# Modulation products of a two-block network: 19 longer runs on TensorE in place of 25, used ahead of their loads' place

## The chip, the cores and the metric

The kernel runs on one core of one Trainium2 chip. The metric is the time of one execution on the device, in microseconds; the figure for the kernel before is the median of three runs.

## The reference, cut to what matters

Two blocks follow each other, each of two layers, on 256 tokens of width 1024. The first is a hybrid of three attentions; the second a hybrid of a convolution, a gated linear attention and a softmax attention, over the 256 tokens and 256 context tokens. Only the second block has a modulation:

```python
def hybrid_layer_2(xs, cs, c, c_ctx, norm_g, w_mod, b_mod, ...):
    shift_x, scale_x, gate_x = jnp.split(jax.nn.silu(c) @ w_mod + b_mod, 3, axis=-1)
    shift_c, scale_c, gate_c = jnp.split(jax.nn.silu(c_ctx) @ w_mod + b_mod, 3, axis=-1)
    hx = rms_norm(xs, norm_g) * (1 + scale_x[:, None]) + shift_x[:, None]
    hc = rms_norm(cs, norm_g) * (1 + scale_c) + shift_c
...
    xs = xs + gate_x[:, None] * merge(px, ya_x, yb_x, yc_x)
```

`w_mod` is 1024 by 3072 in float32 for each of the two layers, 25 MB together, and it meets only two vectors (`c` and `c_ctx`). The vectors are inputs, so these products depend on nothing else in the network and can be made at any time before their results are needed: layer 0's shift and scale before the second block's first normalisation, its gate at that layer's end, layer 1's three later still.

## The kernel before, in words

All other weights come through a stream (`WStream`): a table lists the units, 512 KB each as a rule, in the order of use. A unit is loaded by SyncE's DMA queue into one of four raw buffers (`_dma`, tag `wraw`, line 130), then split by ScalarE (a cast, line 154, giving `wh`) and VectorE (a subtraction, line 155, giving `wl`) into two float32r parts in one of five pairs of buffers (`_split`). Each product of the layers is three matmuls, `mm3` (lines 184 to 186): high by high, high by low, low by high. `get(key)` hands out a split unit and first calls `ahead`, which writes loads for `ad` and splits for `asp` entries of the table ahead of the current one (3 and 2 at first, 6 and 3 from unit 0O00 on).

A unit's name has the layer and the step: in the first block A to I are the input projections and O the output, in the second block AKV, AQ and BQ (attention), Va and Vb (convolution values), GK, GQ, GV, ag, gg, m1 to m3 (gates) and oa, og, oc, o (outputs). 1A2 is the third unit of layer 1's step A.

The modulation weights are 48 more units of that table, in float32 and without a split: layer l, third s (0 shift, 1 scale, 2 gate), k of eight 128-row blocks, 128 by 1024 each, 512 KB. `mod_stream` (line 762) is a generator that makes one unit's products per step. In a unit, four matmuls (line 770) share the moving weights' four quarters of 256 columns among four column groups of the array: the stationary operand is 32 columns wide (128*32 in the trace), and quarter q goes to partitions 32q to 32q+31 of one PSUM accumulator, which is held over the eight units of a third (tag `gm`, five banks for all products of that kind). After the eighth unit ScalarE copies the accumulator out (line 775), two small matmuls against a selection matrix transpose it (line 778, `modt`), and VectorE adds the bias (line 782), and for the scale multiplies with the norm's gain. In the trace each of these float32 matmuls has two records.

`FILL` says where: before unit 1B2 two steps, before 1E2 three, and so on, 25 runs of one to five units, in the order layer 0 scale, shift, gate, then layer 1. In the table the modulation units of a run stand directly ahead of the unit whose `get` makes them.

The order of instructions on an engine is the framework's: it takes ready instructions by the order in which the program wrote them, by a model of their times, so work written later can be placed inside a run and a run inside other work. A manual dependency (`g.wait`) makes an instruction wait for another; `g.after` only fixes an order. A buffer is given to its next owner when all users of the last one are done, and SyncE's queue issues its loads strictly in order.

Of the kernel before, what the change touches and what calls it, by code (L numbers as in the profile page):

```python
# [3 lines left out]

# [6 lines left out]
F32 = mybir.dt.float32  # L11
# [4 lines left out]
OP = mybir.AluOpType  # L16
# [13 lines left out]
TG = 2  # L30
# [8 lines left out]

MORDER = (1, 0, 2)  # L40

FILL = '1B2 2 1E2 3 1D2 3 1F0 2 1G0 2 1H2 1 0Va0 2 0Va1 2 0Va2 2 0GV0 1 0ag0 2 0ag2 2 1GV0 3 1ag0 2 1ag2 2 1A0 1 0BQ2 2 1F2 2 1GK0 1 1B0 1 1A3 5 1C2 1 0ag1 1 1H0 1 0GK0 2'

# [9 lines left out]
def units1():  # L55
    c = lambda *ns: [SPL1[n] for n in ns]
    u = {}
    for key, cols in (('A', c(*_A)), ('B', c('idx_q')), ('C', c('diff_q')), ('D', c('diff_k')), ('E', c('diff_v')),
                      ('H', [(3276, 512)]), ('I', [(3788, 512)])):
        u[key] = [(f'{key}{j}', 2 * j, 2, cols) for j in range(4)]  # L60
    u['A'] = [(f'A{j}', KA[j], KA[j + 1] - KA[j], c(*_A)) for j in range(len(KA) - 1)]
    u['F'] = [(f'F{2 * i + m}', 0, 8, [(SPL1[n][0] + 128 * m, 128)])
              for i, n in enumerate(('fox_q', 'fox_k')) for m in range(2)]
    u['G'] = [(f'G{j}', 4 * j, 4, c('fox_v')) for j in range(2)]
    return [e for st in STEPS[0].split() if st in u for e in u[st]]


def units1o():
    return [(f'O{c}{j}', 2 * j, 2, [(512 * c, 512)]) for c in range(2) for j in range(4)]


def ncols(cols):
    return sum(n for _, n in cols)
# [20 lines left out]
def unit_table(prefix, units, base):  # L94
    t = []
    for key, _, kk, cols in units:
        n = ncols(cols)
        t.append((prefix + key, base, kk, n))
        base += 128 * kk * n
    return t, base  # L100
# [10 lines left out]
class WStream:  # L111
# [46 lines left out]
    def whole(self, key):  # L158

        i = self.idx[key]  # L160
        self.ahead(i)
        key, src, off, kk, n = self.table[i]
        return self.raw.pop(i).rearrange("p (k n) -> p k n", k=kk)

    def ahead(self, i):
        while self.nd < min(len(self.table), i + self.ad + 1):
            self._dma()
        while self.ns < min(len(self.table), i + self.asp + 1):
            if self.table[self.ns][0] in self.f32:
                self.ns += 1  # L170
            else:
                self._split()

    def get(self, key):
        self.ad, self.asp = self.looks.pop(key, (self.ad, self.asp))
        for _ in range(self.fills.pop(key, 0)):
            next(self.stream)
        i = self.idx[key]
        self.ahead(i)
        return self.spl[i]  # L180

# [551 lines left out]
def units_mod():  # L733
    return [(f'mod{s}{k}', k, 1, [(D * s, D)]) for s in MORDER for k in range(8)]
# [24 lines left out]
TAPG = ((0, 0, 6, 4), (3, 3, 14, 10))  # L759


def mod_stream(g, l, W):

    nc, sp, pp = g.nc, g.sp, g.pp
    for s in MORDER:
        ps = pp.tile([128, 256], F32, name=f'mod{l}{s}', tag='gm', bufs=g.GM)
        for k in range(8):
            w = W.whole(f'{l}mod{s}{k}')
            for q in range(4):
                nc.tensor.matmul(ps[32 * q:32 * q + 32], g.cz[:, k // 2, 2 * (k % 2):2 * (k % 2) + 32],  # L770
                                 w[:, 0, 256 * q:256 * q + 256], start=k == 0, stop=k == 7)
            if k < 7:
                yield
        r = sp.tile([128, 256], F32, name=f'modr{l}{s}', tag='tg', bufs=TG)
        nc.scalar.copy(r, ps)
        pt = pp.tile([128, 2, 4, 2], F32, name=f'modt{l}{s}', tag='at', bufs=g.AT)
        for i in range(2):
            nc.tensor.matmul(pt[:, i].rearrange("p q w -> p (q w)"), r[:, 128 * i:128 * i + 128], g.sel8,
                             start=True, stop=True)
        ks = slice(8 * s, 8 * s + 8)  # L780
        v = lambda t: t.rearrange("p (q i) w -> p q i w", q=4)
        nc.vector.tensor_add(v(g.mod[l][:, ks, :]), pt.rearrange("p i q w -> p q i w"),
                             v(g.bmod[l][:, ks, None].to_broadcast([128, 8, 2])))
        if s == 1:

            nc.vector.scalar_tensor_tensor(g.modA[l], g.mod[l][:, ks, :], 1.0,
                                           g.ng[l][:, :, None].to_broadcast([128, 8, 2]), op0=OP.add, op1=OP.mult)
        yield


# [42 lines left out]
def new_hT(g, l):  # L833
    return [[g.k8([128, 4, 512], f'hT{s}{i}_{l}', F32R) for i in range(2)] for s in 'hl']
# [874 lines left out]
def table(src, prefix, units):  # L1709
    t, _ = unit_table(prefix, units, 0)  # L1710
    return [(k, src, o, kk, n) for k, o, kk, n in t]
# [12 lines left out]
def program(ctx, tc, ins, out, parts=(1, 2)):  # L1724
    g = setup(ctx, tc, ins)
    nc = g.nc
    mods = sum((table(ins[f'wm_{l}'], f'{l}', units_mod()) for l in range(2)), [])
    f32 = {e[0] for e in mods}
    fs = FILL.split()
    fills = {k: int(n) for k, n in zip(fs[::2], fs[1::2])}  # L1730
    seq = []
    if 1 in parts:
        for l in range(2):
            us = units1()
            if l == 0:
                seq += [(f'0{k}', None, 0, kk, ncols(c)) for k, _, kk, c in us[:len(KA) - 1]]
                us = us[len(KA) - 1:]
            seq += table(ins[f'w1_{l}'], f'{l}', us) + table(ins[f'w1o_{l}'], f'{l}', units1o())
    for l in range(2):
        t2 = tables2(ins, l)  # L1740
        o = [t2[f'{l}{k}'] for k in order2(l)]
        if l == 0:

            o = o[:7] + [(f'0BQ{i}', *e[1:]) for i, e in enumerate(o[3:7])] + o[7:]
            o += [(f'0p{i}', *e[1:]) for i, e in enumerate(o[-8:])]
        seq += o
    tab, m = [], 0
    for e in seq:
        n = fills.get(e[0], 0)
        tab += mods[m:m + n] + [e]  # L1750
        m += n
    assert m == len(mods)
    ls = LOOK.split()
    looks = {k: (int(a), int(b)) for k, a, b in zip(ls[::3], ls[1::3], ls[2::3])}
    W = WStream(g, tab, looks, f32, fills)
    W.stream = itertools.chain(mod_stream(g, 0, W), mod_stream(g, 1, W))

    xsp = g.dram.tile([128, 2048], F32, name='xsp')

    def loaded(src, nm, key=None):  # L1760

        t = g.k8([128, 8, 256], nm)
        d = nc.sync.dma_start(t, src.rearrange("p (k t) -> p k t", k=8))
        if key is not None:
            g.after(d, W.loads.get(key, W.last))
        return t

    def spill(t):
        nc.sync.dma_start(xsp.rearrange("p (k t) -> p k t", k=8), t)

    def load_res():
        return loaded(xsp, 'xT', '0o1'), loaded(ins['ctxt'], 'ctxT', '0o1')
    hT0 = []

    def ctx_prep():
        hT0.extend(new_hT(g, 0))
        norm_prep(g, 0, [(loaded(ins['ctxt'], 'ctx0', HOOK[2] if 1 in parts else None), 0)], hT0, 0, 256)

    def x_prep(tb, c, pt):

        x = g.t2([128, 4, 128], f'npx{tb}{c}')
        for i in range(4):
            k = 4 * c + i
            if i in NPA:
                nc.scalar.activation(x[:, i], pt[:, i], AF.Identity, scale=g.modA[0][:, k, 1:2], bias=g.mod[0][:, k, 1:2])
            else:
                nc.vector.tensor_scalar(x[:, i], pt[:, i], g.modA[0][:, k, 1:2], g.mod[0][:, k, 1:2],
                                        op0=OP.mult, op1=OP.add)
        hh, hl = (t[c][:, :, 256 + 128 * tb:384 + 128 * tb] for t in hT0)
        nc.scalar.copy(hh, x)  # L1790
        nc.vector.tensor_sub(hl, x, hh.bitcast(F32))
    if 1 in parts:
        xTh, xTl = load_x(g, ins, W)
        setup1(g, ins, W)
        W.hooks[HOOK[3]] = lambda: setup_mod(g, ins, W)
        st = block1(g, 0, xTh, xTl, lambda: load_xtok(g, ins, W), W, False)
        block1(g, 1, *st, W, True, ctx_prep, spill, x_prep)
    setup2(g, ins)
    rope2_tables(g, 0)
    hT1 = []  # L1800

    def then(xT):
        hT1.extend(new_hT(g, 1))
        norm_prep(g, 1, [(xT, 1)], hT1, 0, 256)
    xT, cT = block2(g, 0, hT0, load_res, W, then=then)
    rope2_tables(g, 1)
    norm_prep(g, 1, [(cT, 0)], hT1, 0, 256)
    block2(g, 1, hT1, lambda: (xT, None), W, out=out)
# [22 lines left out]
```

## Time and profile before

| | |
|---|---|
| median of three runs | 1191.99 us (1191.82 to 1192.95) |
| the profiled execution | 1192.62 us |
| its span | 1190.8 us |
| TensorE busy | 1168.5 us, 98% |
| VectorE, ScalarE busy | 921.1 us, 569.5 us |
| DMA | 171.33 MB, 144 GB/s on average |

Busy time of TensorE is the union of modelled intervals: a matmul's row begins at its issue and ends when its result is written, so rows overlap and the cost of an instruction is read from the distance between starts. PE is TensorE's matmuls, PEld its weight loads, DVE VectorE, ACT ScalarE, SP SyncE.

### The profile page before, as it was taken

What the parts mean: (1) busy time and instruction counts of PE and PEld (TensorE: products, weight loads), DVE (VectorE), ACT (ScalarE), POOL (GpSimd) and SP (SyncE); (2) the same over time, 40 slices, a digit from 0 to 9 for tenths busy, and PEclk for the clock granted to TensorE, in tenths of its full rate; (3) what the DMA queues carried; (4) which work ended last, traced back from release to release, by engine and by line L of the source; (5) the groups of instructions that cost most, each with busy time, mean ns of one, the idle gap of its engine ahead of it and who ended that gap; (6) DMA issues with size and microseconds to landing.
All of it is one profiled execution on the core that took longest, in us unless ns stands there. A gap on an engine that the chain in (4) does not pass through costs nothing.

```text
span 1190.8 us, 20632 instructions
## 1 busy us (share of the span) xinstructions
PE 1168.5 (98%) x8024; PEld 975.7 (82%) x8024; DVE 921.1 (77%) x2051; ACT 569.5 (48%) x1024; POOL 11.2 (1%) x42
## 2 busy tenths in 40 slices
PE   8999999999999999999999999999999999999998
PEld 6788777677887777767887888888999778999998
DVE  6996766967799859989545986755799897896984
ACT  5556634456555433247444422433455534855552
POOL 0000000000000000000000000000000000000000
PEclk9999999999999999999999999999999999999999
DMA  7634566465555642024221232325545333554552
GB/s 263 224 125 127 186 207 225 155 229 195 177 194 181 230 137 89 19 73 145 68 84 59 89 100 78 106 89 177 178 142 186 96 107 123 179 162 127 174 176 72
DMA packets 47538, 171.33 MB, mean 144 GB/s; under 512 B 5260, under 2 KB 5900, under 8 KB 46672
## 3 DMA queue, kind: packets, MB, share of 16 engines
q1 hardware_dynamic: 47440, 170.01, 43.7%
q8 instruction: 63, 1.03, 0.3%
q14 instruction: 35, 0.29, 0.1%
HBM read 167.89 MB, written 2.10 MB: 143 GB/s over the span
## 4 chain that ended last, share of the span: by engine, by line
PE 76%; DVE 11%; DMA 6%; ACT 5%; issue 2%; SPq 0%; ACTq 0%; DVEq 0%
PE f0m L186 3%; PE f0m L185 3%; PE f0m L184 3%; PE f1m L186 2%; PE f1m L184 2%; PE f1m L185 2%; PE po L185 1%; PE po L186 1%; PE po L184 1%; PE mod L770 1%; PE go L186 1%; PE go L185 1%; PE go L184 1%; PE yog L186 1%; PE yoc L186 1%
## 5 line engine op out<-in xcount | busy, mean ns | idle before, releaser
L1012 DVE SCALAR_TENSOR_TENSOR ucv<-up,par,ucv 128x512 f32<-128x512 f32 (+1 forms) x240 | 147.3, 614 | 2.8
L184 PE MATMUL f0m<-hTh,wh_0m 128*128 128x512 f32 x192 | 75.1, 391 | 0.0
L185 PE MATMUL f0m<-hTl,wh_0m 128*128 128x512 f32 x192 | 75.1, 391 | 0.0
L186 PE MATMUL f0m<-hTh,wl_0m 128*128 128x512 f32 x192 | 74.8, 390 | 0.0
L184 PE MATMUL f1m<-hTh,wh_1m 128*128 128x256 f32 x192 | 54.9, 286 | 0.1
L186 PE MATMUL f1m<-hTh,wl_1m 128*128 128x256 f32 x192 | 54.8, 286 | 0.0
L185 PE MATMUL f1m<-hTl,wh_1m 128*128 128x256 f32 x192 | 54.5, 284 | 0.0
L154 ACT CAST wh_0m<-wr_0m 128x1024 fp32r<-128x1024 f32 x24 | 25.1, 1047 | 55.9 <-PE f0m L185 14.5
L155 DVE TENSOR_TENSOR wl_0m<-wr_0m,wh_0m 128x1024 fp32r<-128x1024 f32 x24 | 29.3, 1222 | 18.2 <-ACT wh_0m L154 18.1
L184 PEld LDWEIGHTS f0m<-hTh,wh_0m 128*128 128x128 f32 x192 | 36.1, 188 | 7.4
L185 PEld LDWEIGHTS f0m<-hTl,wh_0m 128*128 128x128 f32 x192 | 36.1, 188 | 7.3
L186 PEld LDWEIGHTS f0m<-hTh,wl_0m 128*128 128x128 f32 x192 | 36.1, 188 | 7.3
L184 PEld LDWEIGHTS f1m<-hTh,wh_1m 128*128 128x128 f32 x192 | 36.8, 191 | 0.5 <-ACT wh_1m L154 0.3
L186 PEld LDWEIGHTS f1m<-hTh,wl_1m 128*128 128x128 f32 x192 | 36.7, 191 | 0.2 <-DVE wl_1m L155 0.2
L185 PEld LDWEIGHTS f1m<-hTl,wh_1m 128*128 128x128 f32 x192 | 36.8, 191 | 0.1
L154 ACT CAST wh_1m<-wr_1m 128x1024 fp32r<-128x1024 f32 x24 | 24.9, 1049 | 24.4 <-PE f1m L185 7.6
L155 DVE TENSOR_TENSOR wl_1m<-wr_1m,wh_1m 128x1024 fp32r<-128x1024 f32 x24 | 29.3, 1221 | 8.6 <-ACT wh_1m L154 8.4
L155 DVE TENSOR_TENSOR wl_0o<-wr_0o,wh_0o 128x1024 fp32r<-128x1024 f32 x8 | 9.8, 1224 | 13.2 <-ACT wh_0o L154 13.2
L1413 DVE SCALAR_TENSOR_TENSOR xT<-po,mod,xT 128x256 f32<-128x256 f32 x16 | 7.7, 483 | 14.3 <-PE po L186 14.3
L185 PE MATMUL po<-mgl,wh_0o 128*128 128x256 f32 x64 | 18.2, 285 | 0.0
L186 PE MATMUL pp<-mgh,wl_0p 128*128 128x256 f32 x64 | 18.2, 284 | 0.0
L185 PE MATMUL pp<-mgl,wh_0p 128*128 128x256 f32 x64 | 18.2, 284 | 0.0
(1857 smaller groups left out, 3960.6 us busy)
## 6 DMA issues: line engine op xcount, KB each, us to landing
wr_0mod<-in_wm_dram SPq DMA_DIRECT2D x24, 512.0 KB, 4.5
wr_1mod<-in_wm_dram SPq DMA_DIRECT2D x24, 512.0 KB, 3.7
wr_0m<-in_w_dram SPq DMA_DIRECT2D x24, 512.0 KB, 3.5
wr_1m<-in_w_dram SPq DMA_DIRECT2D x24, 512.0 KB, 3.5
wr_0O<-in_w1o_dram SPq DMA_DIRECT2D x8, 512.0 KB, 3.6
wr_1O<-in_w1o_dram SPq DMA_DIRECT2D x8, 512.0 KB, 3.6
wr_0o<-in_wo_dram SPq DMA_DIRECT2D x8, 512.0 KB, 3.6
wr_0p<-in_wo_dram SPq DMA_DIRECT2D x8, 512.0 KB, 3.7
```

Source lines behind the costliest of these rows:

```text
L154: g.nc.scalar.copy(wh, r)
L155: g.nc.vector.tensor_sub(wl, r, wh.bitcast(F32))
L184: nc.tensor.matmul(out, lh, rh, start=start, stop=False)
L185: nc.tensor.matmul(out, lh, rl, start=False, stop=False)
L186: nc.tensor.matmul(out, ll, rh, start=False, stop=stop)
L770: nc.tensor.matmul(ps[32 * q:32 * q + 32], g.cz[:, k // 2, 2 * (k % 2):2 * (k % 2) + 32], w[:, 0, 256 * q:256 * q + 256], start=k == 0, st ...
L1012: yield nc.vector.scalar_tensor_tensor(o, src, dw[:, i, j:j + 1], o, op0=OP.mult, op1=OP.add)
L1413: nc.vector.scalar_tensor_tensor(r[:, f, :], ps[:, :256], g.mod[l][:, 16 + f, w:w + 1], r[:, f, :], op0=OP.mult, op1=OP.add)
```

## The change

The 48 units are taken in 24 pairs, the two of a pair being the same k of two thirds (`MODS`: scale and shift of layer 0; gate of layer 0 and scale of layer 1; shift and gate of layer 1). A pair's eight matmuls fill the two halves of one accumulator of 512 columns, so there are three accumulators, copies and groups of transposes (eight records, four matmuls) in place of six. The list of runs has 19 entries, 14 of one pair and 5 of two. In the table a run's loads now stand one or two units behind the unit whose `get` makes the products. `get` issues the loads up to the run's last one and hands that load to the generator, and the first matmul of the run waits for it. `ahead` counts only units that are split, so modulation units no longer use up the look-ahead, and `whole` no longer calls it.

```diff
-FILL = '1B2 2 1E2 3 1D2 3 1F0 2 1G0 2 1H2 1 0Va0 2 0Va1 2 0Va2 2 0GV0 1 0ag0 2 0ag2 2 1GV0 3 1ag0 2 1ag2 2 1A0 1 0BQ2 2 1F2 2 1GK0 1 1B0 1 1A3 5 1C2 1 0ag1 1 1H0 1 0GK0 2'
+FILL = (('1A2', 1, 1), ('1B1', 1, 1), ('1E0', 1, 1), ('1E3', 1, 1), ('1C2', 1, 1), ('1D2', 1, 1), ('1F1', 1, 1), ('1H0', 1, 1), ('0BQ3', 1, 2), ('0Va2', 1, 2), ('0Va3', 1, 1), ('0GK0', 1, 1), ('0GQ1', 2, 2), ('0GV2', 2, 2), ('0ag1', 2, 2), ('0ag3', 1, 1), ('0m3_3', 1, 1), ('0m3_6', 1, 1), ('0gg1', 1, 1))
+MODS = (((0, 1), (0, 0)), ((0, 2), (1, 1)), ((1, 0), (1, 2)))
...
     def whole(self, key):
 
         i = self.idx[key]
-        self.ahead(i)
+        while self.nd <= i:
+            self._dma()
...
+    def behind(self, i, n):
+
+        while n and i < len(self.table) - 1:
+            i += 1
+            n -= self.table[i][0] not in self.f32
+        return i
+
     def ahead(self, i):
-        while self.nd < min(len(self.table), i + self.ad + 1):
+        while self.nd < min(len(self.table), self.behind(i, self.ad) + 1):
             self._dma()
-        while self.ns < min(len(self.table), i + self.asp + 1):
+        while self.ns < min(len(self.table), self.behind(i, self.asp) + 1):
...
-        for _ in range(self.fills.pop(key, 0)):
-            next(self.stream)
         i = self.idx[key]
+        if key in self.fills:
+            n, last = self.fills.pop(key)
+            while self.nd <= self.idx[last]:
+                self._dma()
+            self.go = self.loads[last]
+            for _ in range(n):
+                next(self.stream)
         self.ahead(i)
...
-def mod_stream(g, l, W):
+def mod_stream(g, W):
...
-    for s in MORDER:
-        ps = pp.tile([128, 256], F32, name=f'mod{l}{s}', tag='gm', bufs=g.GM)
+    for n, two in enumerate(MODS):
+        ps = pp.tile([128, 512], F32, name=f'mod{n}', tag='gm', bufs=g.GM)
         for k in range(8):
-            w = W.whole(f'{l}mod{s}{k}')
-            for q in range(4):
-                nc.tensor.matmul(ps[32 * q:32 * q + 32], g.cz[:, k // 2, 2 * (k % 2):2 * (k % 2) + 32],
-                                 w[:, 0, 256 * q:256 * q + 256], start=k == 0, stop=k == 7)
+            ws = [W.whole(f'{l}mod{s}{k}') for l, s in two]
+            for h in range(2):
+                for q in range(4):
+
+                    m = nc.tensor.matmul(ps[32 * q:32 * q + 32, 256 * h:256 * h + 256],
+                                         g.cz[:, k // 2, 2 * (k % 2):2 * (k % 2) + 32],
+                                         ws[h][:, 0, 256 * q:256 * q + 256], start=k == h == 0, stop=k == 7,
+                                         skip_group_check=True)
+                    if h == q == 0 and W.go is not None:
+
+                        g.wait(m, W.go)
+                        W.go = None
             if k < 7:
                 yield
-        r = sp.tile([128, 256], F32, name=f'modr{l}{s}', tag='tg', bufs=TG)
+        r = sp.tile([128, 512], F32, name=f'modr{n}', tag='tg', bufs=TG)
         nc.scalar.copy(r, ps)
-        pt = pp.tile([128, 2, 4, 2], F32, name=f'modt{l}{s}', tag='at', bufs=g.AT)
-        for i in range(2):
+        pt = pp.tile([128, 4, 4, 2], F32, name=f'modt{n}', tag='at', bufs=g.AT)
+        for i in range(4):
...
+    for k, late, n in FILL:
+        at[keys[keys.index(k) + late]] = mods[m:m + 2 * n]
+        m += 2 * n
+        fills[k] = n, mods[m - 1][0]
...
     for e in seq:
-        n = fills.get(e[0], 0)
-        tab += mods[m:m + n] + [e]
-        m += n
+        tab += at.get(e[0], []) + [e]
```

## Rows read from the trace of the kernel before

**Rows 1.** Page, part 1: busy us (share of the span) xinstructions.

```profile
PE 1168.5 (98%) x8024; PEld 975.7 (82%) x8024; DVE 921.1 (77%) x2051; ACT 569.5 (48%) x1024; POOL 11.2 (1%) x42
```

**Rows 2.** Page, part 4, the chain that ended last: share of the span.

```profile
PE 76%; DVE 11%; DMA 6%; ACT 5%; issue 2%; SPq 0%; ACTq 0%; DVEq 0%
```

**Rows 3.** Busy time by stage: us, PE PEld DVE ACT POOL (xinstructions), PEclk, DMA share, GB/s.

```profile
160.00:303.00 143.00, 135.90 (x956) 100.07 (x955) 103.52 (x268) 71.17 (x167) 0.54 (x6) 1.00 0.62 208
...
550.00:700.00 150.00, 148.31 (x979) 122.09 (x978) 102.70 (x176) 70.37 (x126) 0.00 (x0) 1.00 0.26 81
```

**Rows 4.** The chain in order of time, 245 to 262 us: start, us, what.

```profile
249.79 1.04 PE mod L770 x16
...
250.85 5.50 DMA wr_1F<-in_w_dram
...
256.38 1.06 ACT wh_1F L154
...
259.89 1.14 DVE wl_1F L155
```

**Rows 5.** Waits of SyncE's queue: us in total, times, longest us.

```profile
SPq L130 <- PE mod L770: 90.4, 25, 14.2
```

**Rows 6.** PE's timeline, modulation pieces: start, us, line, operation, records [idle before].

```profile
161.65 0.63 PE L770 MATMUL mod<-wr_0mod,cz 128*32 128x256 f32 x4
...
236.06 1.50 PE L770 MATMUL mod<-wr_0mod,cz 128*32 128x256 f32 x24
237.49 0.73 PE L184 MATMUL g1D<-wh_1D,xTh 128*128 128x512 f32 x2
...
963.48 0.63 PE L770 MATMUL mod<-wr_1mod,cz 128*32 128x256 f32 x6
964.05 0.50 PE L184 MATMUL t1GV<-wh_1GV,hTh 128*128 128x512 f32 x1
...
1004.65 1.07 PE L770 MATMUL mod<-wr_1mod,cz 128*32 128x256 f32 x16
```

**Rows 7.** PE's timeline around a run of one unit.

```profile
221.04 0.40 PE L186 MATMUL g1C<-wh_1C,xTl 128*128 128x512 f32 x1
221.37 0.64 PE L770 MATMUL mod<-wr_0mod,cz 128*32 128x256 f32 x8
221.94 0.50 PE L184 MATMUL g1C<-wh_1C,xTh 128*128 128x512 f32 x1
222.28 0.40 PE L185 MATMUL g1C<-wl_1C,xTh 128*128 128x512 f32 x1
```

**Rows 8.** PE's timeline around a run of two units.

```profile
534.71 0.39 PE L185 MATMUL f0ag<-hTl,wh_0ag 128*128 128x512 f32 x1
534.93 0.39 PE L186 MATMUL f0ag<-hTh,wl_0ag 128*128 128x512 f32 x1
535.25 1.07 PE L770 MATMUL mod<-wr_1mod,cz 128*32 128x256 f32 x16
536.25 0.50 PE L184 MATMUL f0ag<-hTh,wh_0ag 128*128 128x512 f32 x1
536.59 0.39 PE L185 MATMUL f0ag<-hTl,wh_0ag 128*128 128x512 f32 x1
```

**Rows 9.** PE's timeline, the two waits at modulation places.

```profile
169.71 0.62 PE L770 MATMUL mod<-wr_0mod,cz 128*32 128x256 f32 x2 [0.66 <-DMA wr_0mod<-in_wm_dram]
...
406.28 0.50 PE L184 MATMUL f0Va<-hTh,wh_0Va 128*128 128x512 f32 x1 [0.85 <-ACT wh_0Va L154]
```

**Rows 10.** Loads into wr_0mod, from issue to landing.

```profile
DMA to landing us min/median/max: 3.5/4.5/7.5
```

**Rows 11.** PE's timeline, one group of transposes behind an accumulator.

```profile
189.04 0.61 PE L778 MATMUL modt<-cst,modr 128*128 128x8 f32 x4
```

**Rows 12.** Busy time by stage at the start: columns as in rows 3.

```profile
7.60:10.00 2.40, 0.42 (x2) 0.03 (x1) 0.69 (x1) 1.48 (x2) 0.00 (x0) 1.00 1.01 412
10.00:14.40 4.40, 3.92 (x11) 3.12 (x12) 4.19 (x5) 2.96 (x4) 0.00 (x0) 0.64 1.03 411
```

More of the change, by code (lines that the diff above doesn't have):

```diff
@@ L1 @@
-import itertools
 import math
@@ L779, in mod_stream @@
                              start=True, stop=True)
[L780 to L787, printed above, removed]
+        for h, (l, s) in enumerate(two):
+            ks = slice(8 * s, 8 * s + 8)
+            v = lambda t: t.rearrange("p (q i) w -> p q i w", q=4)
+            nc.vector.tensor_add(v(g.mod[l][:, ks, :]), pt[:, 2 * h:2 * h + 2].rearrange("p i q w -> p q i w"),
+                                 v(g.bmod[l][:, ks, None].to_broadcast([128, 8, 2])))
+            if s == 1:
+                nc.vector.scalar_tensor_tensor(g.modA[l], g.mod[l][:, ks, :], 1.0,
+                                               g.ng[l][:, :, None].to_broadcast([128, 8, 2]), op0=OP.add, op1=OP.mult)
@@ L1726, in program @@
     nc = g.nc
-    mods = sum((table(ins[f'wm_{l}'], f'{l}', units_mod()) for l in range(2)), [])
+    mods = [{e[0]: e for e in table(ins[f'wm_{l}'], f'{l}', units_mod())} for l in range(2)]
+    mods = [mods[l][f'{l}mod{s}{k}'] for two in MODS for k in range(8) for l, s in two]
     f32 = {e[0] for e in mods}
-    fs = FILL.split()
-    fills = {k: int(n) for k, n in zip(fs[::2], fs[1::2])}
     seq = []
@@ L1746, in program @@
         seq += o
-    tab, m = [], 0
+    keys = [e[0] for e in seq]
+    fills, at, m = {}, {}, 0
+    for k, late, n in FILL:
+        at[keys[keys.index(k) + late]] = mods[m:m + 2 * n]
+        m += 2 * n
+        fills[k] = n, mods[m - 1][0]
+    assert m == len(mods)
+    tab = []
     for e in seq:
-        n = fills.get(e[0], 0)
-        tab += mods[m:m + n] + [e]
-        m += n
-    assert m == len(mods)
+        tab += at.get(e[0], []) + [e]
     ls = LOOK.split()
@@ L1755, in program @@
     W = WStream(g, tab, looks, f32, fills)
-    W.stream = itertools.chain(mod_stream(g, 0, W), mod_stream(g, 1, W))
+    W.stream = mod_stream(g, W)
     xsp = g.dram.tile([128, 2048], F32, name='xsp')
```

## The prediction, made before the change was run

> **What bounds the kernel now.** I read the page's engine table first: TensorE (PE) is busy for 1168.5 of 1190.8 us [rows 1], so some 22 us are left in which it stands idle. The chain that ended last says the same less sharply: 76% PE, 11% VectorE (DVE), 6% DMA, 5% ScalarE (ACT) [rows 2]. Then the stages. Half of the modulation work stands in 160 to 303 us, and there PE is busy for 135.90 of 143.00 us; at 550 to 700 us it is 148.31 of 150.00, with the DMA engines at 0.26 [rows 3]. So time that PE no longer needs is mostly gained. The exception is 160 to 303 us: there the chain runs through the ring of four raw load buffers, from a modulation run (249.79) to the load that it let go (250.85, 5.50 us), to ACT's cast (1.06) and DVE's subtraction (1.14) [rows 4]. SyncE's queue waits 90.4 us in all, 25 times, for a buffer that a modulation product still holds [rows 5]: a consumer that comes late holds back the next weights.
>
> **What a run costs on PE.** The timeline of PE shows the 48 units (8 records each: four matmuls, two records to one) in 35 unbroken pieces, although the table asks for 25 runs: the framework's order cuts seven of the runs. The pieces are 19 of at most one unit, 12 of two units, and four of 24, 24, 22 and 18 records; the first, a long one, the last of the small and the last of all stand in [rows 6].
> One unit: the products on either side start at 221.04 and 221.94, 0.90 us apart, where neighbours elsewhere are 0.22 apart (534.71 to 534.93), and the one after follows 0.34 later instead of 0.22. That is 0.68 + 0.12 = 0.80 us [rows 7, 8]. Two units: 534.93 to 536.25 is 1.32, and again 0.34: 1.10 + 0.12 = 1.22 us [rows 8]. A unit more is 0.42, and 0.38 is paid per piece whatever its length. A three-unit piece agrees (1.43 us to the next start, two units 1.00), and a piece of only six records costs what a whole unit does (963.48 to 964.05: 0.57) [rows 6]. Four units are therefore 1.22 + 2 x 0.43 = 2.08 us, an estimate.
>
> **The change, part by part.**
> *Fewer, longer runs.* Before: 19 x 0.80 + 12 x 1.22 + (1.65 + 1.65 + 1.54 + 1.33) = 15.2 + 14.6 + 6.2 = 36.0 us. After, if no run is cut: the new table has 19 entries (the title says 20), 14 of one pair and 5 of two pairs: 14 x 1.22 + 5 x 2.08 = 27.5 us. That is 8.5 us less. Nearly all of it lies in 160 to 303 us, where 18 pieces of 18.5 us become 8 of 9.8 us; later 17 pieces of 17.5 us become 11 of 17.7 us.
> *Cuts.* Nothing in the diff forbids other ready work inside a run, except that the first matmul now waits until all loads of the run have landed, which takes away cuts of the kind at 169.71 [rows 9]. A cut costs from 0.38 (two pieces of a unit or more) to 0.7 (a two-record piece split off). Ten cuts in 25 runs before would be 7 or 8 in 19; some of them came from late loads, so I take 5 x 0.5 = 2.5 us.
> *Waits that go.* The only two PE waits at modulation places, 0.66 us for a modulation load and 0.85 us for the cast of 0Va's weights behind two runs [rows 9]: 1.5 us.
> *Wait that is added.* A run's first matmul waits for the run's last load, and everything behind it on PE waits with it. A run of two units leaves two buffers to the others, and since its products now stand ahead of a unit whose load stands ahead of theirs, the load that takes over its buffer is a unit or two further from its use than before: 0. A run of four units fills all four raw buffers; the next unit's load can start only when the run's first unit is done. At 0Va2 that is 0Vb2: the load lands in 4.5 us (median of the modulation loads, 3.5 to 7.5) [rows 10], plus 1.06 + 1.14 for the split [rows 4] is 6.7 us, up to 9.7. The cover is the rest of the run (some 1.3 us) and 0Va2's own 24 products at 0.22 to 0.23, 5.5 us: 6.8. So between 0 and 2.9 us of wait; the median lies at the zero end, and I take 0.4 for each of the five such runs, 2.0 us. 0BQ3 has 30 products as cover, the three others further units and attention work.
> *Tails.* Six groups of four transposing records (0.61 us) [rows 11] become three of eight: no more than 3.7 us before, 1.8 to 3.7 after; I take 0.5 us of gain. ACT makes three copies of 512 columns for six of 256, DVE the same eight instructions: nothing, since PE only meets them through these tails.
> *Loads.* 48 loads of 512 KB before and after, by the same SyncE queue. 160 to 303 us loses eight of them; the layer-1 ones of 900 to 1010 us move to before 700 us, where the DMA engines are at 0.26 [rows 3]. Counting the look-ahead in units without the modulation only moves the places in the program at which splits are written: 0, and in 160 to 303 us rather a gain. One of the five PSUM accumulators is now held through 550 to 700 us; in 160 to 303 us it is held already, and no PE wait there is for a bank: 0.
> *Sum.* -8.5 + 2.5 - 1.5 + 2.0 - 0.5 = -6.0 us against the profiled execution's own 1192.62 us (span 1190.8 and 1.8 around it), so 1186.6. That execution stands 0.6 above the median of the runs shown (1191.99): as a median 1186.0.
>
> **The rivals.**
> 1. *The gain is eaten where it is made* (about 1191). For it: in 160 to 303 us the chain is the load ring [rows 4], and small pieces there also fill PE while an attention step is late (the stage has 7.1 us of idle [rows 3]); or the order cuts the new runs so often that there are 35 pieces again, so that the change doesn't do what it says. If the 8.7 us of that stage are lost, 17.7 for 17.5 us is left. Against it: that stage has eight loads fewer, and their consumers come sooner.
> 2. *The ring is relieved as well* (about 1181). No cuts: 8.5 + 1.5 + 0.5 = 10.5 us gained; a third of the 7.1 us of idle on top would be 1179.
> 3. *Slower: the four-unit runs starve PE* (about 1198). Place: the first weight cast behind 0BQ3, 0Va2, 0GQ1, 0GV2 and 0ag1. Price: the upper 2.9 us in each, 14.5 us, for the 2.0 in the sum: -6.0 + 12.5 = +6.5. It decides when the load and split take over 8.5 us there; the median of 6.7 speaks against it, the 5.50 us load in a busy stretch [rows 4] for it.
> 4. *Such a wait also slows PE's clock* (about 1206). PE was busy for 0.42 of 2.40 us while it waited for the first weights, and the 4.40 us behind had a granted clock of 0.64, between the levels of 1.2 and 2.4 GHz [rows 12]: 0.36 x 4.4 = 1.6 us lost. Five starved runs would add 8 us to rival 3. The Trainium skill (TensorE: Matmul & The Clock Gate, "HAM oscillation — how this bites in real kernels") has it that a wait for DMA between bursts of matmuls puts the engine back to half clock, which speaks against any run that waits for all its loads. By that rule the trace agrees only for the start: at the 0.66 us of wait [rows 9] the granted clock of the stage stayed 1.00 [rows 3], so this gets a small chance.
>
> **How the numbers follow.** Forecast with its neighbourhood (1182 to 1189.5) 0.62, rival 2 0.11, rival 1 0.15, rival 3 0.10, rival 4 0.02. The range takes the forecast, rival 2 and most of rival 1: 1179.5 to 1191.8; the upper ends of the waits and of the cuts reach 1191 too. A measurement of this kernel tells about 0.2%, 2.4 us, from no change: faster is 0.62 + 0.11 = 0.73, the same 0.15, slower 0.12.
>
> **What would show it.** In the changed profile: PE's timeline with 19 to 25 modulation pieces, of 16 or 32 records, 1.00 and about 1.86 us to the next start; their summed price near 30 us by the arithmetic above; the stage up to 1H3's end some 8 us shorter, the part after it about even, since the runs at 926 to 1005 us only come earlier. The forecast is wrong if PE shows waits for wh_0Vb, wh_0GV or wh_0ag, or for wr_0mod and wr_1mod, of more than some 4 us together, if the pieces are over 30, or if PE's idle time grows by what its busy time loses.

## The result, and the profile after the change

The changed kernel takes 1198.91 us (median of 7 runs, 1194.87 to 1200.75), against 1192.43 us for 7 runs of the kernel before on the same chip (one of these took 2900.65 us, which doesn't move the median). The ratio is 1.0052, 95% interval 1.0036 to 1.0067. It is slower by about half a per cent, outside the range given, and on the side that had a chance of 0.12. The profiled execution took 1197.96 us with a span of 1196.2 us.

The page after, part 1 (as [rows 1]) and the first line of part 4 (as [rows 2]):

```profile
PE 1170.6 (98%) x8024; PEld 978.4 (82%) x8024; DVE 921.0 (77%) x2051; ACT 569.1 (48%) x1021; POOL 11.1 (1%) x42
...
PE 78%; DVE 12%; ACT 5%; DMA 3%; issue 2%; SPq 0%; ACTq 0%; DVEq 0%
```

These averages hide what happened. TensorE is busy for 2.1 us *more* and stands idle for 25.6 us instead of 22.3 (span less busy time). The same work on PE took longer, and only a look at stages tells where. The table follows five tiles in the two PE timelines, each by the end of its last product (start plus length of its last record). The last two columns are what each stage gained or lost. The sixth experiment below stands beside it: its profile reaches the end of the first row at the same moment as the one before, and it has no stall.

| end of | before | after | exp. 6 | after, this stage | exp. 6, this stage |
|---|---|---|---|---|---|
| fo01t (half of block 1) | 134.55 | 132.78 | 134.54 | -1.77 | -0.01 |
| go, layer 1 (block 1 done) | 342.59 | 332.32 | 333.76 | -8.50 | -8.82 |
| f0Vb | 433.78 | 434.92 | 425.95 | **+11.41** | +1.00 |
| f0gg | 671.47 | 682.17 | 673.05 | +9.56 | +9.41 |
| f1m | 1152.50 | 1157.85 | 1149.58 | -5.35 | -4.50 |

The first row has no modulation work in it: the two profiles differ there from their first tile on (see the end of this document). The second row is the gain that was forecast. The third is the accident, and it is one place. (The fourth and fifth have modulation work moved from the fifth into the fourth, so they count together.) The stages around it, in the columns of [rows 3]:

```profile
365.00:370.00 5.00, 0.67 (x3) 0.14 (x1) 4.61 (x27) 1.03 (x4) 0.00 (x0) 0.84 0.03 12
370.00:375.00 5.00, 1.97 (x5) 1.42 (x6) 4.83 (x25) 0.57 (x2) 0.00 (x0) 0.50 0.06 15
375.00:382.00 7.00, 5.89 (x37) 2.04 (x35) 5.58 (x30) 1.57 (x5) 0.00 (x0) 0.50 0.42 136
382.00:390.00 8.00, 8.00 (x38) 6.45 (x36) 7.23 (x15) 5.57 (x8) 0.00 (x0) 1.00 0.88 310
```

PE is busy for 0.67 and 1.97 of 5 us. Its granted clock falls to 0.50, that is 1.2 GHz, and stays there while it works again. Meanwhile VectorE (DVE) is busy nearly all the time, and the DMA engines at 0.03 and 0.06. PE's timeline names the waits (start, us, instruction, and in brackets the idle time and who ended it):

```profile
367.37 0.33 PE L974 MATMUL akt<-cst,kb 128*128 128x128 f32 x1 [2.02 <-DVE kb L945]
...
370.67 0.42 PE L960 MATMUL lrt<-cst,kb 128*96 128x128 f32 x1 [2.98 <-DVE kb L953]
...
373.45 0.79 PE L198 MATMUL t0BQ<-wl_0BQ,hTh 128*128 128x512 f32 x1 [2.35 <-DVE wl_0BQ L155]
...
377.05 1.06 PE L785 MATMUL mod<-wr_0mod,cz 128*32 128x256 f32 x2 [1.11 <-DMA wr_1mod<-in_wm_dram]
```

Four waits of 8.46 us together, and behind them the run of four units at 0BQ3. In the 12 us from 370 to 382 PE's 7.86 busy us at 0.50 hold 3.93 us of work. Not all of that is lost: until 377.05 PE waits for DVE and for a load, whatever its own pace. From there to 382 it is busy for all 4.95 us, and half of these, some 2.5 us, come on top of the waits. Read one by one, the waits blame DVE three times. The queue of SyncE and two rows of DVE tell a different story:

```profile
358.65 0.33 SPq L130 DMA_DIRECT2D wr_0mod<-in_wm_dram  x1
360.05 0.33 SPq L130 DMA_DIRECT2D wr_1mod<-in_wm_dram  x1
361.32 0.33 SPq L130 DMA_DIRECT2D wr_0mod<-in_wm_dram  x1
373.46 0.33 SPq L130 DMA_DIRECT2D wr_1mod<-in_wm_dram  x1
...
379.79 0.33 SPq L130 DMA_DIRECT2D wr_0Va<-in_w_dram  x1
...
360.08 1.22 DVE L155 TENSOR_TENSOR wl_0BQ<-wr_0BQ,wh_0BQ 128x1024 fp32r<-128x1024 f32 x1
372.18 1.22 DVE L155 TENSOR_TENSOR wl_0BQ<-wr_0BQ,wh_0BQ 128x1024 fp32r<-128x1024 f32 x1
```

Three loads of the run go out by 361.32. The fourth goes out 12 us later, at the moment the subtraction of BQ3's split ends and gives back a raw buffer. That subtraction stands 12.1 us behind the one before it, because DVE works through the k and q chain of block 2 in between. PE has little else to do meanwhile: the first load of 0Va, the weights that come next, stands behind the fourth load and goes out at 379.79, when the run has begun. In the kernel before, the same two subtractions (of BQ2 and BQ3) were late too, with the same chain between them, 8.2 us apart:

```profile
373.82 1.22 DVE L155 TENSOR_TENSOR wl_0BQ<-wr_0BQ,wh_0BQ 128x1024 fp32r<-128x1024 f32 x1
...
382.06 1.22 DVE L155 TENSOR_TENSOR wl_0BQ<-wr_0BQ,wh_0BQ 128x1024 fp32r<-128x1024 f32 x1
```

There PE's longest wait between 360 and 390 us is 0.39 us. In the changed kernel the chain that ended last says it in four rows:

```profile
372.26 1.15 DVE wl_0BQ L155
373.46 3.55 DMA wr_1mod<-in_wm_dram
377.05 1.06 PE mod L785 x2
...
378.73 3.48 PE mod L785 x28
```

### The profile page after: what moved, and what is told of

It is laid out like the page before. It is cut to its first block, busy times and chain, and to the rows that moved or that the text cites. A ratio compares the mean times of both kernels' runs of the same rounds, so it can differ in the third digit from the quotient of the medians.

```text
span 1196.2 us, 20660 instructions
## 1 busy us (share of the span) xinstructions
PE 1170.6 (98%) x8024; PEld 978.4 (82%) x8024; DVE 921.0 (77%) x2051; ACT 569.1 (48%) x1021; POOL 11.1 (1%) x42
## 4 chain that ended last, share of the span: by engine, by line
PE 78%; DVE 12%; ACT 5%; DMA 3%; issue 2%; SPq 0%; ACTq 0%; DVEq 0%
PE f0m L199 4%; PE f0m L197 4%; PE f0m L198 4%; PE mod L785 2%; PE f1m L198 2%; PE f1m L197 2%; PE f1m L199 2%; PE po L198 1%; PE po L199 1%; PE po L197 1%; PE go L197 1%; PE go L199 1%; PE go L198 1%; PE yoc L199 1%; PE yoc L197 1%
## 5 line engine op out<-in xcount | busy, mean ns | idle before, releaser
L785 PE MATMUL mod<-wr_0mod,cz 128*32 128x256 f32 x192 | 18.5, 407 | 1.1 <-DMA wr_1mod<-in_wm_dram 1.1
L785 PE MATMUL mod<-wr_1mod,cz 128*32 128x256 f32 x192 | 18.3, 404 | 0.0
```

The lines of the kernel that those rows point to most:

```text
L785: m = nc.tensor.matmul(ps[32 * q:32 * q + 32, 256 * h:256 * h + 256], g.cz[:, k // 2, 2 * (k % 2):2 * (k % 2) + 32], ws[h][:, 0, 256 * q:2 ...
```

## The experiments

Times are medians, ratios are against runs of the kernel before on the same chip. Every edit is made to the changed kernel. FILL's entries are: unit at which a run is used, units by which its loads stand further on, number of pairs. Of FILL only the entries that change, and some beside them, are shown.

**1. The run taken off BQ3.**

```
-('0BQ3', 1, 2), ('0Va2', 1, 2)
+('0Va0', 1, 1), ('0Va1', 1, 1), ('0Va2', 1, 2)
```

> The four units at 0BQ3 are used as two runs of one pair at 0Va0 and 0Va1, each loaded one unit further on; nothing else changes. Theory (the 11.4 us lost between 360 and 435 us come from the run at 0BQ3, which holds up unit BQ3's own split and products): that stretch gets back about 11 us, less one more cut of 0.5, so about 1187.5 us (1186 to 1190), no wait of TensorE over 1.5 us between 360 and 390 us, clock 1.00 there. Rival (the loss lies in four-unit runs as such and in the nine cuts spread over the kernel): only a fifth of it or less comes back, 1195 us or more.

Measured: 1188.26 us, ratio 0.9972 (0.9955 to 0.9989). The longest wait of PE between 364 and 384 us is 0.38 us, and the granted clock is 1.00 in each of the four windows shown above. So the loss was in this place. The cuts that the change has elsewhere are all still there.

**2. The run of four moved one unit, whole.**

```
-('0BQ3', 1, 2)
+('0Va0', 1, 2)
```

> The same four units stay one run of four, used at 0Va0 and loaded one unit further on. Theory (place): about 1187 us (1186 to 1190), as in the run that splits them, since the place and not the length decides. Rival (length: a run of four keeps TensorE from the products that follow and its four loads hold the queue): 1194 us or more, 6 us or more behind the split version.

Measured: 1195.27 us, ratio 1.0034 (1.0019 to 1.0048), the rival's number. The first theory failed here: the place alone does not decide. The profiled execution, of 1191.79 us, is the fastest of the eight. PE's timeline, SyncE's queue and DVE of this run, around the stall:

```profile
376.59 1.06 PE L785 MATMUL mod<-wr_0mod,cz 128*32 128x256 f32 x2 [5.37 <-DMA wr_1mod<-in_wm_dram]
...
362.46 0.33 SPq L130 DMA_DIRECT2D wr_0mod<-in_wm_dram  x1
372.92 0.33 SPq L130 DMA_DIRECT2D wr_1mod<-in_wm_dram  x1
...
361.22 1.22 DVE L155 TENSOR_TENSOR wl_0BQ<-wr_0BQ,wh_0BQ 128x1024 fp32r<-128x1024 f32 x1
371.63 1.22 DVE L155 TENSOR_TENSOR wl_0Va<-wr_0Va,wh_0Va 128x1024 fp32r<-128x1024 f32 x1
```

BQ3 is now split early, at 361.22, and its products run on. But the fourth load again goes out 10.5 us behind the third, this time when the split of Va0 ends, which is now the late one. In both stalls it is the split of the unit loaded just ahead of the run.

**3. The loads of the run at BQ3 one unit further on.**

```
-('0BQ3', 1, 2)
+('0BQ3', 2, 2)
```

> The run of four stays at 0BQ3 and in the same place of TensorE's order, but its loads are issued two units behind instead of one, so the split of BQ3 stands 44 instructions earlier in VectorE's order. Theory in its narrow form (the late subtraction of BQ3's split is what TensorE waits for): the wait of 2.35 us goes and with it most of the half-clock stretch, about 1189 us (1187 to 1192). Rival (the run's place in TensorE's own order, with two transposes ahead of it that wait for VectorE and its first matmul that waits for the fourth load): the idle time stays or grows by a load's wait, 1197 us or more.

Measured: 1197.76 us, ratio 1.0059 (1.0042 to 1.0077): the rival's number. BQ3's subtraction now ends by 362.32, and nothing is gained. The narrow form of the theory (PE waits for the late subtraction) has fallen. The wait has become a single one:

```profile
376.42 1.06 PE L785 MATMUL mod<-wr_0mod,cz 128*32 128x256 f32 x2 [8.91 <-DMA wr_1mod<-in_wm_dram]
```

**4. No wait for the load at BQ3.**

```
-            self.go = self.loads[last]
+            self.go = None if key == '0BQ3' else self.loads[last]
```

> The run at 0BQ3 keeps its place and its loads, but its first matmul no longer waits for the fourth load (the runs elsewhere still do). Theory in its narrow form (late subtraction): the subtraction stays late, the wait for the split stays, only the 1.1 us wait for the load and part of the half-clock stretch go: 1194 us (1192 to 1197). Rival (the wait itself, which pushes the whole run behind the transposes in TensorE's order): about 1187 us (1186 to 1190).

Measured: 1188.25 us, ratio 0.9969 (0.9954 to 0.9984): the rival again. BQ3's subtraction is as late as in the changed kernel (369.73 us, 12.1 behind the third), and yet there is no stall. PE's timeline and SyncE's queue:

```profile
362.63 0.64 PE L785 MATMUL mod<-wr_0mod,cz 128*32 128x256 f32 x8
...
367.32 0.62 PE L785 MATMUL mod<-wr_1mod,cz 128*32 128x256 f32 x2
...
358.92 0.33 SPq L130 DMA_DIRECT2D wr_0mod<-in_wm_dram  x1
363.33 0.33 SPq L130 DMA_DIRECT2D wr_1mod<-in_wm_dram  x1
```

The run's first unit is multiplied at 362.63, as soon as it is there. That frees a buffer, and the fourth load goes out at 363.33. From these four runs comes the theory that the next ones test. There are four raw buffers. A run that waits for four loads holds three of them and needs the fourth, which is that of the unit ahead of it. If the split of that unit stands behind a long piece of DVE work, PE waits for DVE with three loaded units in hand.

**5. The wait put on the third load.** At 0BQ3 alone:

```
-            self.go = self.loads[last]
+            self.go = self.loads[self.table[self.idx[last] - (key == '0BQ3')][0]]
```

> The run of four at 0BQ3 stays one run, but its first matmul waits for the third of its four loads instead of the fourth. Theory, formed on the four runs before: there are four raw buffers, so the fourth load takes over the buffer of the unit loaded just ahead of the run; that unit is split behind the k and q work of VectorE (some 10 us late), and a run that waits for its fourth load waits for this split, while it holds the three other buffers itself. Three loads need no such buffer: the stall goes, no wait for a modulation load over 1.5 us, 1188 us (1186 to 1190). Rival (any wait of a run of four in this place puts the whole run behind VectorE's chain): half of the stall or more stays, 1192 us or more.

Measured: 1189.24 us, ratio 0.9965 (0.9950 to 0.9981). A run of four with a wait in the same place, and no stall: the wait is 0.65 us. The first unit's products start at 366.83, the fourth load goes out at 367.53, and the last unit's products follow as a second piece.

**6. Two runs of one pair, both with their wait.**

```
-('0BQ3', 1, 2)
+('0BQ3', 1, 1), ('0Va0', 1, 1)
```

> The run of four at 0BQ3 becomes one pair at 0BQ3 and one pair at 0Va0; both first matmuls wait for their last load as in the changed kernel. Theory (fourth load, fourth buffer): two loads need no buffer of a unit that is not yet split, so 1188 us (1186 to 1190), though a run with a wait stands at 0BQ3 as before. Rival (the wait at this place, whatever the run's length): 1194 us or more.

Measured: 1188.79 us, ratio 0.9957 (0.9937 to 0.9977). Two loads need no buffer of a unit that is not yet split. PE's longest wait between 345 and 400 us is 1.5 us.

**7. No run waits for its loads.** The manual dependence on the last load is left out everywhere.

> No run waits for its last load, anywhere. Theory (only the run at 0BQ3 is hurt by its wait, and the other waits cost nothing and keep the runs together): the stall goes, and three more pieces at 0.4 us come, 1189.5 us (1187 to 1191.5), some 1 us behind the kernel that drops this one wait. Rival (the waits elsewhere, at the four other runs of four, cost time too): 1186 us or less, 2 us or more ahead of it.

Measured: 1191.56 us, ratio 0.9991 (0.9974 to 1.0007). Neither number came: it is 0.06 us slower than the theory allowed. The stall at BQ3 is gone here too, but in the profiled execution another stands further on, where without waits the order had become a different one. (That execution took 1195.05 us, 3.5 above the median, so the others may not have all of it.) PE's timeline:

```profile
431.10 0.80 PE L1066 MATMUL at000s<-k,at000q 128*128 128x256 f32 x2 [4.00 <-ACT at000q L1057]
```

The stages around it, in the columns of [rows 3]:

```profile
425.00:430.00 5.00, 2.09 (x21) 0.90 (x19) 1.23 (x1) 2.11 (x3) 0.00 (x0) 1.00 0.49 159
430.00:435.00 5.00, 3.90 (x13) 3.42 (x14) 2.81 (x4) 1.04 (x2) 0.00 (x0) 0.50 0.96 350
435.00:440.00 5.00, 5.00 (x22) 3.60 (x22) 3.41 (x8) 1.19 (x2) 0.00 (x0) 0.81 0.17 68
```

So the waits at the other places are not what costs time, and this run does not say that they gain any: what it has instead is another late step, and half clock behind it.

**8. Many cuts.** As experiment 1, with all modulation runs written at a priority 5 steps ahead of their place.

```
-            for _ in range(n):
-                next(self.stream)
+            with self.g.tc.high_priority(5):
+                for _ in range(n):
+                    next(self.stream)
```

> The two runs at 0Va0 and 0Va1 as in the first experiment, and in addition all modulation runs are written at a priority 5 steps ahead of their place, which makes the order mix them with the products around: 87 pieces of modulation matmuls instead of 29, 44 of them or more a single matmul. The number of matmuls is the same. Theory (a change between the wide products and the 32-column ones costs 0.4 us a piece on TensorE, however it is filled): 58 pieces more are 22 us, 1210 us (1203 to 1218). Rival (pieces are nearly free where other work stands between them, and the forecast's gain from fewer pieces was something else): less than 6 us more, 1194 us or less.

Measured: 1220.93 us, ratio 1.0225 (1.0196 to 1.0254). By the ratios that is 0.0253 x 1192, 30 us more than experiment 1 for 58 pieces more: 0.52 us a piece, above the 0.4 of the theory and outside its range. PE's timeline shows what a single matmul between wide products costs:

```profile
412.74 0.62 PE L786 MATMUL mod<-wr_0mod,cz 128*32 128x256 f32 x2
413.29 0.49 PE L199 MATMUL f0Va<-hTl,wh_0Va 128*128 128x512 f32 x1
413.72 0.62 PE L786 MATMUL mod<-wr_0mod,cz 128*32 128x256 f32 x2
414.26 0.49 PE L200 MATMUL f0Va<-hTh,wl_0Va 128*128 128x512 f32 x1
```

Part 1 of its page has the sum:

```profile
PE 1202.8 (99%) x8024; PEld 982.0 (81%) x8024; DVE 921.1 (76%) x2051; ACT 568.9 (47%) x1021; POOL 11.1 (1%) x42
```

One modulation matmul and one product take 0.98 us (412.74 to 413.72) where the product alone takes 0.22 [rows 8]. So a lone matmul adds 0.76 us, nearly what a whole unit of four does (0.80). So nearly all of the price is that of the change to and fro. Of the 87 pieces 64 are single matmuls.

**9 and 10. A fifth raw buffer, and its control.** The table and the wait are untouched. Five raw buffers do not fit beside the rest, so both kernels have one large block buffer less.

```
-KN = (5, 3, 4, 5, 2, 12, 6, 5, 2, 4)
+KN = (5, 3, 5, 5, 2, 11, 6, 5, 2, 4)    (experiment 9)
+KN = (5, 3, 4, 5, 2, 11, 6, 5, 2, 4)    (experiment 10)
```

> The changed kernel as it is, run of four at 0BQ3 and its wait for the fourth load included, with five raw buffers instead of four; the space comes from the tag of the large block buffers, 11 instead of 12. Theory (the fourth load lacks a buffer): with a fifth buffer it needs none that waits for BQ3's split, so the stall goes: 1188 us (1185 to 1191), no wait between 355 and 380 us over 1.5 us, and 8 us or more ahead of the control with four raw buffers and 11 large ones. Rival (the wait for four loads at this place, buffers or not): like the control, within 3 us.

> The control for the fifth buffer: the changed kernel with four raw buffers and 11 large block buffers. Theory: the stall at 0BQ3 is there as in the changed kernel, 1199 us (1196 to 1203) where the twelfth large buffer was not needed; if it was, both this and the kernel with five raw buffers lose the same on top.

Measured: 1190.92 us with five (ratio 0.9977, 0.9964 to 0.9991) and 1200.49 us with four (1.0059, 1.0041 to 1.0077), 9.6 us apart. The control has the four waits of the changed kernel again (2.05, 2.98, 2.36 and 1.27 us). With the fifth buffer, PE's timeline, SyncE's queue and DVE are:

```profile
370.49 0.64 PE L785 MATMUL mod<-wr_0mod,cz 128*32 128x256 f32 x8 [0.85 <-DMA wr_1mod<-in_wm_dram]
...
364.33 0.33 SPq L130 DMA_DIRECT2D wr_0mod<-in_wm_dram  x1
365.61 0.33 SPq L130 DMA_DIRECT2D wr_1mod<-in_wm_dram  x1
...
376.85 1.22 DVE L155 TENSOR_TENSOR wl_0BQ<-wr_0BQ,wh_0BQ 128x1024 fp32r<-128x1024 f32 x1
```

The fourth load goes out 1.3 us behind the third and does not ask for BQ3's split, which is late as ever (376.85) and now disturbs nobody. The stage that ends with f0Vb takes 92.8 us with five buffers, 101.8 in the control and 91.2 before. That settles the cause. (Experiment 9 loses time elsewhere: in block 1 its profile has a wait of 3.09 us for ACT, with half clock behind it, and this is no part of the stall at BQ3.)

**11 and 12. Fewer cuts.** Experiment 6, and the ten pairs behind 0GK0 as five runs of four units, where the order was expected to cut none of them.

```
-('0GQ1', 2, 2), ('0GV2', 2, 2), ('0ag1', 2, 2), ('0ag3', 1, 1), ('0m3_3', 1, 1), ('0m3_6', 1, 1), ('0gg1', 1, 1)     (both)
+('0m3_1', 1, 2), ('0m3_3', 1, 2), ('0m3_5', 1, 2), ('0m3_7', 1, 2), ('0gg1', 1, 2)     (experiment 11)
+('0gg1', 1, 2), ('0m2_1', 1, 2), ('0m2_3', 1, 2), ('0m2_5', 1, 2), ('0m2_7', 1, 2)     (experiment 12)
```

> One pair each at 0BQ3 and 0Va0 as in the sixth experiment, and the ten pairs behind 0GK0 as five runs of four units at m3_1, m3_3, m3_5, m3_7 and gg1 of layer 0, loaded one unit behind, where the order cuts none of them: 20 pieces instead of 28. Theory (a piece costs 0.4 to 0.5 us, a run of four is harmless where the splits of the units ahead are not late): 8 pieces fewer are 3 to 4 us, 1185 us (1183 to 1187.5), no wait for a modulation load over 1.5 us. Rival (a run of four with its wait stalls TensorE wherever it stands): 1192 us or more. Rival (small pieces filled idle time in the attention stage, so they were nearly free there): as the sixth experiment, 1188 to 1190 us.

> As the run before it, with the five runs of four at gg1, m2_1, m2_3, m2_5 and m2_7 of layer 0. The same 20 pieces stand later, in products that keep TensorE busy. Theory: as the run before it within 1.5 us (1183 to 1188), since only the number of pieces and of starved runs counts, not the place. Rival (a place with more idle time on TensorE hides part of a piece): 2 us or more apart.

Measured: 1186.43 us, ratio 0.9943 (0.9925 to 0.9961), and 1185.47 us, ratio 0.9938 (0.9920 to 0.9957). Both beat the kernel before and the changed one, and have the lowest medians of the study. They lie within 1 us of each other, as the theory said. No run waits for a load, so a run of four harms nothing where the splits ahead of it are on time. In experiment 12 all five runs stay whole, 20 pieces; in experiment 11 the order cuts two of them (into 2 and 30 records, 4 and 28), so it has 22. A whole run of experiment 12 is one row of 32 records, then the next product follows:

```profile
667.46 1.93 PE L785 MATMUL mod<-wr_1mod,cz 128*32 128x256 f32 x32
669.32 0.50 PE L197 MATMUL f0m<-hTh,wh_0m 128*128 128x512 f32 x1
```

From the end of f0Vb to that of f1m, in the columns of [rows 3], experiment 6 (28 pieces) and then 12:

```profile
426.00:1149.00 723.00, 717.47 (x5249) 614.45 (x5248) 565.61 (x1125) 330.73 (x540) 6.99 (x22) 1.00 0.38 122
```

```profile
427.00:1147.00 720.00, 714.24 (x5249) 615.00 (x5248) 565.90 (x1125) 331.57 (x540) 7.00 (x22) 1.00 0.39 123
```

Eight pieces fewer save 3.2 us of PE's busy time, 0.40 each, and the six fewer of experiment 11 save 2.3 (715.16 us over 424 to 1145 us), 0.39 each: the theory's price. By the ratios the two kernels are 1.7 and 2.3 us ahead of experiment 6, less than the 3 to 4 us expected, but the intervals overlap. The busy times of the whole pages (1166.0 us in experiment 6, 1163.7 in experiment 12) would give 0.29 a piece. They hold stretches at different clocks: experiment 12 has 0.50 over 226 to 229 us, behind a wait of 1.81 us, and experiment 6 has 1.00 there. In experiment 8 a piece costs 0.6 us of busy time (1202.8 against 1165.8 in experiment 1, and 1.7 of these 37.0 us are half clock at the start: 35.3 us for 58 pieces).

## Why the prediction was wrong

**What bounds the kernel, and the gain of block 1: right.** TensorE is the bound, and the half with the most modulation work is where fewer pieces paid. The sum there was 18.5 to 9.8 us less, 0.66 us of wait, and cuts against it; the stage gained 8.50 us in the changed kernel and 8.82 in experiment 6.

**The wait that is added: the step that failed.** The text had the fact in hand ("a run of four units fills all four raw buffers") and looked only behind the run: the load of the *next* unit, and whether 0BQ3's 30 products cover it. It priced that at 0.4 us a run. The changed kernel has no wait for any such load. The fault lies ahead of the run: its own fourth load needs the buffer of the unit loaded just before, so "all loads have landed" quietly includes "the unit ahead is split". At 0Va2, 0GQ1, 0GV2 and 0ag1 that costs nothing. At 0BQ3 the split waits behind some 11 us of k and q work on DVE. The rows of before that would have shown it are DVE's order in 374 to 382 us, which was not read. The list of SyncE's waits, of which [rows 5] has the second row, has this kind of wait in its first: loads that wait for a subtraction to give back a raw buffer, here for the m units.

```profile
SPq L130 <- DVE wl_0m L155: 134.7, 22, 13.1
```

Price: 1198.91 against 1188 to 1189 without it, 10 us for a term of 2.0 for all five runs. The signs that the text gave for being wrong did not show it either: PE's waits for the loads that it named are 1.11 us, the pieces are 28, and PE's busy time did not fall.

**Rival 3** named this place among five, and its time (1198) came out almost exactly, but not by its mechanism: four of its places cost nothing, and the fifth cost some 10 us instead of 2.9. **Rival 4**, given 0.02, is a part of what happened: the granted clock fell to 0.50 in and behind the stall, for some 2.5 us of the loss. The rule of the Trainium skill cited with it (TensorE: Matmul & The Clock Gate, "HAM oscillation — how this bites in real kernels") is borne out at the stalls of this study, of 4.0 us (experiment 7) and more. The doubt drawn from the 0.66 us wait does not reach far. Beside the waits of up to 1.8 us in experiments 1 and 4 the clock stayed 1.00, but in the changed kernel itself it fell to 0.50 behind one of 1.20 us in block 1 (last section).

**Cuts: mis-sized in number.** Five were taken, nine came (28 pieces for 19 entries; the title says 19 too, not the 20 that the prediction has), seven of them behind block 1. So the later stages, forecast at 17.5 before and 17.7 after plus a part of the cuts, came out worse. Summed in the two timelines from each piece's start to the next product's, the pieces there take 14.83 us before (17 pieces, 0.85 us of it the wait for 0Va's cast [rows 9]) and 17.92 in experiment 6 (18 pieces). Without that wait, and with 0.23 us a piece for the neighbours (0.11 ahead and 0.12 behind [rows 7, 8]), that is 17.9 and 22.1, 4.2 us more. The stages themselves lost 1.00 + 9.41 - 4.50 = 5.9 us in experiment 6. This is why, with the stall gone, the gain is 3 to 5 us (ratios 0.9957 to 0.9972) and not the 8.0 that the terms make without the 2.0 of load waits. That the forecast of -6.0 lies close to it is luck: a term of 2.0 for waits that were not there stood in for cuts that were.

**The price of a piece: right.** For a cut the text gave 0.38 us, or up to 0.7 where a lone matmul is split off. Experiments 11 and 12 give 0.39 and 0.40, experiment 8 0.5 to 0.6 for pieces that are mostly single matmuls.

**Waits that go: right, but replaced.** The wait for 0Va's cast [rows 9] is gone. A new one of 1.2 us stands at the first scores of attention (at000s, for ACT's at000q); 0.8 to 1.9 us of it are in ten of the thirteen versions, and account for a part of the 5.9.

**Tails and loads: as said.** The three groups of eight transposes take 1.06, 0.96 and 0.95 us, 3.0 together, within the 1.8 to 3.7 given. The only wait of PE for a modulation load is the 1.11 us at 0BQ3.

## What to carry to other kernels

When a consumer is made to wait for the last of several transfers, count the buffers that it holds meanwhile, and ask who must release the one it still needs. If the run is as long as the ring, the answer is the unit *ahead*, and its release may stand behind other work on another engine. Waiting for one transfer fewer, or a run one buffer shorter than the ring, lets the run go without that dependence. And before two kernels' busy times are compared, look at the granted clock of each stretch: a single stretch at half clock can hide or make up the difference.

## What the runs showed of the hardware

**The clock after a stall.** PE idle for 8.91 us (experiment 3) was followed by 0.54 of full clock over 375 to 382 us, 5.37 us (experiment 2) by 0.58, 4.00 us (experiment 7) by 0.50 over 430 to 435 us; each time it was back at 1.00 within the next 10 us of work. The stall of 8.46 us in the changed kernel, broken by a few short matmuls, was no better: 0.50 over 370 to 382 us. Behind the end of the stall PE's busy time at half clock is 5.0, 4.3, 5.8 and 5.0 us, in the same order, and 3.0 us in the control (experiment 10). Half of it is what each stall cost on top of its idle time, 1.5 to 2.9 us, no more behind the longest than behind the shortest.

Shorter waits went either way. The changed kernel, its clock behind the wait (in the columns of [rows 3]), then experiments 9 and 5:

```profile
206.90 2.07 PE L329 MATMUL is<-ai 64*128 64x256 f32 x8 [1.20 <-ACT ir L333]
...
208.00:211.00 3.00, 3.00 (x9) 1.96 (x7) 2.78 (x7) 1.42 (x2) 0.00 (x0) 0.50 0.54 175
```

```profile
208.75 2.07 PE L329 MATMUL is<-ai 64*128 64x256 f32 x4 [3.09 <-ACT ir L333]
```

```profile
223.97 0.39 PE L419 MATMUL da10s<-fvn,idb 128*128 128x256 bf16 x2 [1.84 <-DVE fvn L358]
```

Behind 1.20 us in the changed kernel the clock was 0.50, and so it was over 208 to 217 us in experiment 9. Behind 1.84 us in experiment 5 it stayed 1.00 (224 to 230 us). So the length of one such wait does not tell.

**One narrow matmul costs what four do.** 0.76 us for one of 256 columns on 32 columns of weights between wide products (experiment 8), 0.80 for four.

**The start varies.** The last product of the first tile, g0A, ended at 20.06 us before, at 18.33 after and at 16.68 in experiment 11, with the same program ahead of it. A part of this is the clock: over 10 to 14.4 us it was 0.64 before [rows 12] and 1.00 in the other two. In the five profiles with a half-clock stretch there (before, experiments 5, 6, 8 and 12) the tile ended at 19.8 to 20.1 us, in the nine others at 16.7 to 18.9. That moves a single profile by up to 3.4 us, more than some of the effects here, and is why stages are compared by their own length and kernels by their medians.
